# Down projections of two MLPs as Strassen products, with a ring of activation operands

## The chip, the cores and the metric

The kernel runs on one NeuronCore of one Trainium2 chip. The metric is the device time of one execution in microseconds. The kernel before took 3331.81 us (median of 3 runs, 3323.62 to 3334.83).

## The reference

A trunk of two layers over 1024 tokens and 16 learned tokens in front, 1040 in all, with 1024 features in float32. Each layer adds a token mixer to the residual stream (gated DeltaNet in the first, mLSTM in the second) and then an MLP:

```python
def squared_relu_mlp(h, w_up, w_down):
    a = jax.nn.relu(h @ w_up)
    return (a * a) @ w_down
...
        h = h + mix
        h = h + squared_relu_mlp(rms_norm(h, ffn_norm[layer]), ff_up[layer], ff_down[layer])
    return h[:, N_META:]
```

`w_up` is 1024 x 4096 and `w_down` 4096 x 1024. The case is about `(a * a) @ w_down` of both layers.

## The kernel before

Everything is kept feature-major: a tile has 128 features on partitions and tokens along the free dimension. The residual stream `hT` is eight such tiles of 1040 tokens in SBUF. Tokens go by halves of 520 and groups of 260. A float32 product is three single-pass matmuls (`mm3`, L105 to L107): each operand is split as hi + lo, the cast to hi on ScalarE and the low part `x - hi` as a subtraction on VectorE or GpSimd, and hi hi + lo hi + hi lo is summed in PSUM.

The stages run in this order: DeltaNet, its output projection, MLP of layer 1 (up, then down), mLSTM, MLP of layer 2. The up projection (`Up`, L933) already works by Strassen-Winograd products: of 2 x 2 blocks seven products instead of eight, each with a sum of weight blocks and a sum of token blocks. Its weight operands are made by `operand` (sums on VectorE L962, cast on ScalarE L978, low part L980). In the first and last few turns of a stage the low part of four of the seven goes to GpSimd (`help`), in the others all are VectorE's. The squared activations go to DRAM, `d_a`, by pairs of feature tiles.

The down projection (`Down`, L1044) is a plain product. It goes over eight blocks of four feature tiles of the activations (`HB`). A tile of 1040 tokens is fetched to `a_st` and split into `act_hi` (ScalarE, L1064) and `act_lo` (VectorE, L1065). For each block and each pair of output tiles, weights of 512 KB are loaded and split (L124 on ScalarE, L125 on GpSimd), and for each output tile and token group twelve matmuls accumulate in one PSUM tile `ps_dn`, which VectorE adds to `hT` (L1084). The last block goes by halves of the tokens: in layer 1 each finished block of `hT` is squared for the next norm (`ToNorm`, L853 to L857) and a finished half is normalised (`apply`, L896 to L902); in layer 2 each finished tile is transposed and written out (`ToOut`, L1187 to L1191), and the first half is one group of 504 tokens, since the 16 learned ones are dropped.

The order on each engine comes from a scheduler that sorts the program's instructions by a model of their times; the program's own order is that of `weave`, one step of every background stream between two pieces of the matmul stream. Tiles are rotated by pools, so a buffer's next writer waits for its last reader.

Of the kernel before, what the change touches and what calls it, by code (L numbers as in the profile page):

```python
# [7 lines left out]
F32 = mybir.dt.float32  # L8
F32R = mybir.dt.float32r
# [21 lines left out]
HB = 4  # L31
ALL = [[(0, G), (G, G)], [(2 * G, G), (3 * G, G)]]
REAL = [[(META, HALF - META)], ALL[1]]
# [15 lines left out]
class Ctx:  # L49
# [52 lines left out]
# Products of float32 operands: each is split as x = hi + lo with 12-bit parts, and  # L102
# hi*hi + hi*lo + lo*hi carries float32's accuracy in three single-pass products.
# [29 lines left out]
def softplus_neg_abs(nc, t, x):  # L133
    """log1p(exp(-|x|)) = 2 atanh(e / (2 + e)) as its series; returned without the factor 2."""
# [59 lines left out]
class GDN:  # L194
    """Gated DeltaNet by halves of the tokens and pairs of value heads.

    With raw (unnormalised) k and q, rk = |k|^-1, the recurrence is solved for y, v_new = beta rk y:
      (I + A) y = v / rk - e^cum k S,   A_ij = (k_i k_j) beta_j rk_j^2 e^(cum_i - cum_j),  i > j
      o ~ e^cum q S + [(q_i k_j) beta_j rk_j^2 e^(cum_i - cum_j)] y
    The norm of q enters through the epsilon of the output's RMS norm alone.  # L200
    Matrices over token pairs are held as [j, i].
    """
# [72 lines left out]
    def norm_in(self):  # L275
        """RMS norm of the first half's tokens."""
# [27 lines left out]
    def h_init(self, cc):  # L304
        """The residual stream of a chunk, feature-major, and the second half's sums of squares."""
# [35 lines left out]
    def norm_pair(self, j):  # L341
        """RMS norm of two feature tiles of the second half."""
# [87 lines left out]
    def column(self, s, ct, out):  # L430
        """Projection, convolution and SiLU of 128 features."""
# [60 lines left out]
    def prep(self, s, idx):  # L492
# [4 lines left out]
        # token-major k, and the norms of k and q  # L497
# [40 lines left out]
        # strictly upper 16 x 16 diagonal blocks, then their inverses by back substitution  # L538
# [13 lines left out]
        # token-major v / rk  # L552
# [22 lines left out]
        # merges 16 -> 32 -> 64 -> 104: with P' = B12^T L1, U12 = -P'^T U2, L = U^T  # L575
# [59 lines left out]
    def scan(self, s):  # L635
# [16 lines left out]
        for ci in range(HC):  # L652
# [31 lines left out]
            # -o, and its RMS norm  # L684
# [77 lines left out]
class OutUnits:  # L762
    """Output projection of the GDN layer, by halves of the tokens and of the heads."""
# [75 lines left out]
class Norm:  # L839
    """RMS norm over the features of the feature-major residual stream, sums of squares kept as it is made."""  # L840

    def __init__(self, c, pool, nw, ss=None):
        self.c, self.nc, self.pool, self.nw = c, c.nc, pool, nw
        self.ss = pool.tile([P, T], F32, tag="ss", name="ss") if ss is None else ss
        self.x, self.summed = [None, None], None
# [3 lines left out]
    def square(self, d, t0, n):  # L849
        nc, ss = self.nc, self.ss[:, t0:t0 + n]  # L850
        x = self.c.hT[:, d, t0:t0 + n]
        if d == 0:
# [6 lines left out]
    def sums(self, hf):  # L859
        """1 / rms of the tokens of a half, with tokens on partitions."""  # L860
# [9 lines left out]
    def rms(self, hf):  # L870
        """1 / rms of the tokens of a half, on all partitions."""
# [4 lines left out]
        r = self.pool.tile([P, 2, G], F32, tag="r", name="nr", bufs=1)  # L876
# [9 lines left out]
    def apply(self, hf, pool):  # L886
        """The normalised tokens of a half as an operand's two parts, by pairs of feature tiles."""
# [46 lines left out]
class Up:  # L934
    """relu(W_up^T x)^2 of all tokens, kept in DRAM, by Strassen-Winograd products: pairs of feature tiles of
    the result, of halves of the contraction and of token groups, a = [f, k] blocks and b = [k, t] blocks."""
    # product, its operand of the tokens
# [17 lines left out]
    def operand(self, raw, name, help):  # L955
        """A block of the weights, or a sum of blocks, as its two parts; the sums take the places of blocks."""
# [26 lines left out]
    def evac(self, i, hs, name, ps, tmp):  # L983
        """u: a11 b11, then the result's common part, then that of its second column; v: that of its second row."""
# [32 lines left out]
    def run(self, jobs):  # L1017
        """jobs: (pair of feature tiles, halves of the tokens, whether GpSimd helps, what to do first)."""
# [25 lines left out]
class Down:  # L1044
    """The residual stream plus W_down^T of the activations, over blocks of HB feature tiles."""

    def __init__(self, c, w_down, acts, after, spans):
        self.c, self.nc, self.w, self.acts, self.after, self.spans = c, c.nc, w_down, acts, after, spans
        self.a, self.pools, self.next = {}, [], []

    def open(self, st, side):
        self.pools.append(self.c.pool(f"acts{len(self.pools)}", HB, st, side=side))

    def fetch(self, j):
        st = self.c.row(j % 2, "a_st")
        self.nc.sync.dma_start(out=st, in_=self.acts[j // 2][:, j % 2].rearrange("p a b c -> p (a b c)"))
        self.next.append(st)

    def load(self, j):
        """A feature tile of the activations as its two parts."""  # L1060
        nc = self.nc
        st = self.next.pop(0)
        hi, lo = self.a[j] = pair(self.pools[j // HB % 2])
        nc.scalar.copy(hi.rearrange("p a b -> p (a b)"), st)  # L1064
        nc.vector.tensor_tensor(lo.rearrange("p a b -> p (a b)"), st, hi.rearrange("p a b -> p (a b)").bitcast(F32),  # L1065
                                op=ALU.subtract)
        if j + 1 < FF // P:
            self.fetch(j + 1)

    def tiles(self, b, dd, parts, last):  # L1070
        nc, c, hT = self.nc, self.c, self.c.hT
        whi, wlo = load_split(c, self.w[b * HB * P:(b + 1) * HB * P, dd * 256:(dd + 1) * 256].rearrange(
            "(h p) f -> p h f", p=P), [P, HB, 256])
        for d2 in range(2):
            d = dd * 2 + d2
            fs = slice(d2 * P, (d2 + 1) * P)
            for hf in parts:
# [545 lines left out]
```

## Time and profile before

| | |
|---|---|
| median of 3 runs | 3331.81 us (3323.62 to 3334.83) |
| span of the profiled execution | 3327.5 us |
| TensorE busy | 3149.4 us, 95% |
| VectorE busy | 1952.4 us, 59% |
| ScalarE busy | 1515.9 us, 46% |
| GpSimd busy | 980.2 us, 29% |
| down projection, layer 1 | 1671 to 2045 us |
| down projection, layer 2 | 2953 to 3321 us |

The profile is of one execution; its span goes from the first to the last instruction, and what lies around it is under the spread of the runs. Engines are PE (TensorE), PEld (its weight loads), DVE (VectorE), ACT (ScalarE), POOL (GpSimd) and SP (the queue of most DMAs). Busy times of operations overlap a little on VectorE, where one starts before the last has ended: the distance between starts is what an operation costs.

### The profile page before, as it was taken

To read this page: it belongs to the slowest core of one execution; us is meant where nothing else is said; L and a number is where in the kernel's file an instruction comes from. 1 tells how busy PE (TensorE), PEld (TensorE's weight loads), DVE (VectorE), ACT (ScalarE), POOL (GpSimd) and SP (SyncE) were. 2 spreads that over 40 slices of the span, in tenths; PEclk is the share of its full clock that TensorE was granted. 3 is DMA by queue.
4 is the path that set the end of the run, shared out by engine and by line. 5 is a ranking of instruction groups with operands and counts; after the bars stand their busy time and mean duration, and the time that the engine had idled before them with its cause. 6 is when DMAs were issued, how large, how long until landed. Compare 5 with 4: busy or idle time off the path is not lost.

```text
span 3327.5 us, 67692 instructions
## 1 busy us (share of the span) xinstructions
PE 3149.4 (95%) x27430; PEld 2981.0 (90%) x27430; DVE 1952.4 (59%) x4336; ACT 1515.9 (46%) x3547; POOL 980.2 (29%) x824
## 2 busy tenths in 40 slices
PE   7899998999999998899999998999999799999999
PEld 6898887888898898899999998988988799999998
DVE  6777668686676547876644437232336977553332
ACT  4565566656665543555521114433334455541112
POOL 4544444343443434200122224211123400022222
PEclk9999999999999999999999999999999999999999
DMA  3232222232223472343433222211132244343323
GB/s 95 70 85 79 68 76 81 67 91 66 80 74 94 143 213 71 115 131 115 130 115 99 90 65 70 63 52 48 47 90 59 82 132 125 106 144 96 96 90 96
DMA packets 398218, 308.87 MB, mean 93 GB/s; under 512 B 29201, under 2 KB 365242, under 8 KB 397906
## 3 DMA queue, kind: packets, MB, share of 16 engines
q1 hardware_dynamic: 362333, 270.44, 28.0%
q10 hardware_dynamic: 35573, 34.10, 3.0%
q8 instruction: 216, 3.54, 0.4%
q14 instruction: 96, 0.79, 0.1%
HBM read 245.88 MB, written 58.61 MB: 92 GB/s over the span
## 4 chain that ended last, share of the span: by engine, by line
PE 50%; DVE 5%; DMA 1%; ACT 1%; issue 1%; POOL 0%; SPq 0%; DVEq 0%; ACTq 0%; POOLq 0%
PE ps_dn L105 7%; PE ps_dn L107 7%; PE ps_dn L106 7%; PE ps_up L105 6%; PE ps_up L106 6%; PE ps_up L107 6%; PE ps_m L105 2%; PE ps_m L106 2%; PE ps_m L107 2%; PE mpo L1415 1%; PE mpo L1414 1%; DVE ss L857 1%; PE mpk L1377 1%; PE ps_mo L105 1%; PE ps_mo L107 1%
## 5 line engine op out<-in xcount | busy, mean ns | idle before, releaser
L125 POOL TENSOR_TENSOR wlo<-wraw,whi 128x1024 fp32r<-128x1024 f32 (+1 forms) x248 | 599.6, 2418 | 1134.6 <-ACT whi L124 1092.8
L105 PE MATMUL ps_dn<-act_hi,whi 128*128 128x260 f32 (+1 forms) x1792 | 536.7, 300 | 1.3 <-DVE hT L1084 1.2
L105 PE MATMUL ps_up<-xhi,uop 128*128 128x260 f32 x1792 | 511.4, 286 | 27.7 <-DVE up_u L991 10.0
L106 PE MATMUL ps_dn<-act_lo,whi 128*128 128x260 f32 (+1 forms) x1792 | 534.6, 298 | 0.0
L107 PE MATMUL ps_dn<-act_hi,wlo 128*128 128x260 f32 (+1 forms) x1792 | 533.6, 299 | 0.1
L107 PE MATMUL ps_up<-xhi,uop 128*128 128x260 f32 x1792 | 508.6, 284 | 3.2 <-DVE uop L980 3.2
L106 PE MATMUL ps_up<-xlo,uop 128*128 128x260 f32 x1792 | 510.4, 285 | 0.9 <-POOL xlo L927 0.9
L105 PE MATMUL ps_in<-act_hi,whi 128*128 128x260 f32 x1536 | 458.7, 299 | 15.2 <-ACT sz L489 12.4
L124 ACT CAST whi<-wraw 128x1024 fp32r<-128x1024 f32 (+1 forms) x248 | 255.8, 1032 | 472.5 <-PE ps_dn L106 359.9
L106 PE MATMUL ps_in<-act_lo,whi 128*128 128x260 f32 x1536 | 457.7, 298 | 0.0
L107 PE MATMUL ps_in<-act_hi,wlo 128*128 128x260 f32 x1536 | 452.8, 295 | 0.6 <-POOL wlo L125 0.5
L1084 DVE TENSOR_TENSOR hT<-hT,ps_dn 128x260 f32<-128x260 f32 (+1 forms) x448 | 204.5, 461 | 423.3 <-PE ps_dn L107 423.0
L105 PEld LDWEIGHTS ps_up<-xhi,uop 128*128 128x128 f32 x1792 | 341.4, 191 | 31.9 <-ACT uop L978 10.9
L105 PEld LDWEIGHTS ps_dn<-act_hi,whi 128*128 128x128 f32 x1792 | 337.5, 188 | 13.1 <-issue 1.3
L107 PEld LDWEIGHTS ps_dn<-act_hi,wlo 128*128 128x128 f32 x1792 | 338.3, 189 | 11.0 <-POOL mV L1293 0.3
L106 PEld LDWEIGHTS ps_dn<-act_lo,whi 128*128 128x128 f32 x1792 | 338.7, 189 | 10.5
L107 PEld LDWEIGHTS ps_up<-xhi,uop 128*128 128x128 f32 x1792 | 341.2, 191 | 3.8 <-DVE uop L980 3.6
L106 PEld LDWEIGHTS ps_up<-xlo,uop 128*128 128x128 f32 x1792 | 341.6, 191 | 1.4 <-POOL xlo L927 1.3
L105 PEld LDWEIGHTS ps_in<-act_hi,whi 128*128 128x128 f32 x1536 | 297.0, 193 | 21.1 <-ACT sz L489 14.4
L106 PEld LDWEIGHTS ps_in<-act_lo,whi 128*128 128x128 f32 x1536 | 297.2, 193 | 3.9 <-issue 0.2
L107 PEld LDWEIGHTS ps_in<-act_hi,wlo 128*128 128x128 f32 x1536 | 296.7, 193 | 3.9 <-POOL wlo L125 1.1
L105 PE MATMUL ps_m<-act_hi,whi 128*128 128x260 f32 x768 | 224.2, 292 | 5.6 <-ACT mso L1340 2.4
(386 smaller groups left out, 7064.0 us busy)
## 6 DMA issues: line engine op xcount, KB each, us to landing
wraw<-in_gdn_in_dram SPq DMA_DIRECT2D x96, 512.0 KB
wraw<-in_ff_down_dram SPq DMA_DIRECT2D x72, 512.0 KB
a_st<-d_a SPq DMA_DIRECT2D x64, 520.0 KB
d_a<-up_c ACTq DMA_DIRECT2D x88, 260.0 KB
wraw<-in_ff_up_dram SPq DMA_DIRECT2D x42, 512.0 KB
r<-in_ff_up_dram SPq DMA_DIRECT2D x42, 512.0 KB
wraw<-in_gdn_out_dram SPq DMA_DIRECT2D x32, 512.0 KB
wraw<-in_mlstm_in_dram SPq DMA_DIRECT2D x28, 512.0 KB
```

The source lines that it names most:

```text
L105: nc.tensor.matmul(ps, whi, xhi, start=first, stop=False)
L106: nc.tensor.matmul(ps, whi, xlo, start=False, stop=False)
L107: nc.tensor.matmul(ps, wlo, xhi, start=False, stop=last)
L124: nc.scalar.copy(hi, raw)
L125: (lo_engine or nc.gpsimd).tensor_tensor(lo, raw, hi.bitcast(F32), op=ALU.subtract)
L857: nc.vector.tensor_tensor(ss, ss, sq, op=ALU.add)
L1084: nc.vector.tensor_tensor(hT[:, d, t0:t0 + n], hT[:, d, t0:t0 + n], ps, op=ALU.add)
L1377: nc.tensor.matmul(pk[:, i], k[sl, c0 + i], q[sl, c0 + i], start=True, stop=True)
L1414: nc.tensor.matmul(po[:, 0], q[sl, ci], C[sl], start=True, stop=True)
L1415: nc.tensor.matmul(po[:, 1], E[hf][:, j, ci], V[:, ci, j], start=True, stop=True)
```

## The change

Both down projections now go by the same seven products. The contraction (32 feature tiles) is cut into 16 pairs `k`, the output into four pairs `j` of feature tiles (`PAIRS`), the tokens into pairs of groups in each half `hf`. For a pair `k` and a half, `feed` makes seven activation operands: the three blocks that are used as they are and four differences `dt` (VectorE, L1116), each with hi (ScalarE, L1129 to L1132) and lo (VectorE). They stand in a ring of four pairs per half (`RING`). A *turn* is one `j` with two or three pairs `k` (`UPTO`): it loads two rows of weights, makes seven weight operands (sums on VectorE L1162, cast on ScalarE L1177, low part on GpSimd L1178), and runs seven products of two or three `mm3` each. The first and the last round of four `j` go by halves of the tokens, one turn for each, so each makes its operands twice; the four rounds between take both halves in a turn. That is 32 turns of 7 weight operands per layer, 133 operands of 384 columns and 91 of 256. Every product is added from PSUM to `hT` or to a common part `z` (L1223 to L1228); `z` is added to three blocks of `hT` at the end (L1231, L1233). In the second layer all 1040 tokens are computed.

Beside it: six PSUM banks for `ps_dn` instead of four, the norms' bank closed during the stage; the first three pairs of the first half are fed during the last turns of the up projection; the next norm's scratch and the output rows lie in the two row tiles that held other things; the sums of squares start at the first block finished instead of feature tile 0; pools on other sides.

```diff
-    def tiles(self, b, dd, parts, last):
...
-                for t0, n in self.spans[hf]:
-                    gs = slice(t0 - hf * HALF, t0 - hf * HALF + n)
-                    ps = self.psum.tile([P, 512], F32, tag="pj", name="ps_dn")[:, :n]
-                    for j in range(HB):
-                        hi, lo = (x[:, hf, gs] for x in self.a[b * HB + j])
-                        mm3(nc, ps, whi[:, j, fs], wlo[:, j, fs], hi, lo, j == 0, j == HB - 1)
-                    nc.vector.tensor_tensor(hT[:, d, t0:t0 + n], hT[:, d, t0:t0 + n], ps, op=ALU.add)
...
+    RING = 4
+    PAIRS = KT // 2
+    UPTO = (2, 2, 3, 3, 4, 5, 6, 6, 7, 8, 9, 9, 10, 11, 11, 12, 13, 14, 14, 14, 16, 16, 16, 16)
+    OPERAND = {"a11": 0, "a12": 1, "s2": 4, "s3": 5, "s1": 3, "a22": 6, "s4": 2}
+    BANK = {"a11": "x", "a12": "x", "s3": "y", "a22": "y", "s1": "v", "s4": "v", "s2": "u"}
+    BOTH = ("a11", "s3", "a12", "s1", "a22", "s2", "s4")
+    ONE = ("a11", "s3", "s1", "s2", "a12", "a22", "s4")
...
+        for r, upto in enumerate(rounds):
+            split = r in (0, len(rounds) - 1)
+            for parts in ((0,), (1,)) if split else ((0, 1),):
+                for j in range(n):
+                    self.turns.append((j, at[j], upto[j], parts))
+            at = list(upto)
...
+    def feed(self):
...
+        for i, (k, hf) in enumerate(self.loads):
+            if i + 1 < len(self.loads):
+                self.fetch(i + 1)
+            b1, b2 = (r[:, i % 2] for r in self.rows)
+            t = self.dt.tile([P, 4, G], F32, tag="dt", name="dt")
+            sub(t[:, 0], b1[:, 1], b1[:, 0])
+            sub(t[:, 2], b2[:, 1], b1[:, 1])
+            yield
+            sub(t[:, 1], b2[:, 1], t[:, 0])
+            sub(t[:, 3], b2[:, 0], t[:, 1])
...
+            nc.scalar.copy(hi[:, 3:7], t)
+            sub(lo[:, 0], b1[:, 0], hi[:, 0].bitcast(F32))
+            sub(lo[:, 1:3], b2, hi[:, 1:3].bitcast(F32))
+            yield
+            sub(lo[:, 3:5], t[:, 0:2], hi[:, 3:5].bitcast(F32))
+            yield
+            sub(lo[:, 5:7], t[:, 2:4], hi[:, 5:7].bitcast(F32))
...
+    def operand(self, i, name):
...
+        if name == "s3":
+            x = sub(self.dm.tile([P, 3, P], F32, tag="s3", name="s3")[:, :kb], a11, a21)
+            self.raws[i].append(x)
+        elif name == "s1":
+            x = sub(a21, a21, a22, ALU.add)
+        elif name == "s2":
+            x = sub(a11, a22, self.raws[i][4])
+        elif name == "s4":
+            x = sub(a12, a12, a11)
...
+        nc.scalar.copy(w[:, 0:kb], x)
+        nc.gpsimd.tensor_tensor(w[:, kb:2 * kb], x, w[:, 0:kb].bitcast(F32), op=ALU.subtract)
...
+    def product(self, i, u, hf):
...
+        for k in range(kb):
+            hi, lo = (x[:, self.OPERAND[name]] for x in self.x[k0 + k, hf])
+            nc.tensor.matmul(ps, w[:, k], hi, start=begins and k == 0, stop=False, skip_group_check=True)
+            nc.tensor.matmul(ps, w[:, k], lo, start=False, stop=False, skip_group_check=True)
+            nc.tensor.matmul(ps, w[:, kb + k], hi, start=False, stop=k == kb - 1, skip_group_check=True)
...
+            if name == "a11" and k0 == 0:
+                nc.scalar.copy(z, ps)
+            else:
+                nc.vector.tensor_tensor(z, z, ps, op=ALU.add)
+        else:
+            out = place(d, t)[2]
+            nc.vector.tensor_tensor(out, out, ps, op=ALU.add)
...
+        for i, (j, k0, k1, parts) in enumerate(self.turns):
+            while self.todo < len(self.loads) and self.need[self.todo] <= i:
+                next(self.feeder)
...
+            for u in range(7):
+                self.ahead(i, u, 3)
+                for hf in parts:
+                    self.product(i, u, hf)
+                    if self.todo < len(self.loads) and self.room[self.todo] <= i:
+                        next(self.feeder)
...
-        down.psum = c.pool("pd", 4, pst, space=PSUM)
+        down.psum = c.pool("pd", 6, pst, space=PSUM)
```

How the instructions move is seen at two places of layer 1. First VectorE in the middle of the down projection. Before, about one block (`hT` are the evictions, `act_lo` the low parts of the activations):

```order
L1084 TENSOR_TENSOR hT<-hT,ps_dn 128x260 x27
L1065 TENSOR_TENSOR act_lo<-a_st,act_hi 128x1040 x2
L1084 TENSOR_TENSOR hT<-hT,ps_dn 128x260 x4
L1065 TENSOR_TENSOR act_lo<-a_st,act_hi 128x1040
L1084 TENSOR_TENSOR hT<-hT,ps_dn 128x260
```

And now, a part of one turn (`dt` and `dlo` are a pair's differences and low parts, `s`, `r` and `wraw` the weight sums):

```order
L1225 TENSOR_TENSOR z<-z,ps_dn 128x260
L1162 TENSOR_TENSOR s_23499<-wraw,r_23441 128x384
L1225 TENSOR_TENSOR z<-z,ps_dn 128x260
L1162 TENSOR_TENSOR r_23441<-r_23441 128x3x128
L1228 TENSOR_TENSOR hT<-hT,ps_dn 128x260
L1116 TENSOR_TENSOR dlo<-a_st,dhi 128x260
L1116 TENSOR_TENSOR dlo<-a_st,dhi 128x520
L1162 TENSOR_TENSOR wraw<-wraw 128x3x128
L1228 TENSOR_TENSOR hT<-hT,ps_dn 128x260
L1116 TENSOR_TENSOR dlo<-dt,dhi 128x520 x2
L1116 TENSOR_TENSOR dlo<-a_st,dhi 128x260
L1225 TENSOR_TENSOR z<-z,ps_dn 128x260
```

Where runs of up to 27 evictions followed each other with a few low parts between, evictions, weight sums and activation operands now alternate. Second GpSimd, from the end of the up projection into the down projection. Before (`uop` are low parts of the up projection, `wlo` of the down weights, 35 in a row):

```order
L980 TENSOR_TENSOR uop<-s_21322,uop 128x512
L980 TENSOR_TENSOR uop<-r_21262,uop 128x512
L980 TENSOR_TENSOR uop<-wraw,uop 128x512
L125 TENSOR_TENSOR wlo<-wraw,whi 128x1024
L1293 MEMSET mV_26441 104x10
L1293 MEMSET mV_26442 104x10
L125 TENSOR_TENSOR wlo<-wraw,whi 128x1024 x35
```

And now, with the first turn's seven operands `dop` and the first of the second's:

```order
L979 TENSOR_TENSOR uop<-s_21324,uop 128x512
L979 TENSOR_TENSOR uop<-r_21257,uop 128x512
L979 TENSOR_TENSOR uop<-wraw,uop 128x512
L1178 TENSOR_TENSOR dop<-wraw,dop 128x256
L1178 TENSOR_TENSOR dop<-s_21527,dop 128x256
L1178 TENSOR_TENSOR dop<-r_21522,dop 128x256
L1178 TENSOR_TENSOR dop<-wraw,dop 128x256 x2
L1178 TENSOR_TENSOR dop<-r_21522,dop 128x256
L1178 TENSOR_TENSOR dop<-wraw,dop 128x256
L1178 TENSOR_TENSOR dop<-s_21612,dop 128x256
```

36 long subtractions in the stage have become 224 short ones, each of which a product waits for.

## Rows read from the trace of the kernel before

**Rows 1.** The page, parts 1 and 4: busy time by engine, chain.

```profile
PE 3149.4 (95%) x27430; PEld 2981.0 (90%) x27430; DVE 1952.4 (59%) x4336; ACT 1515.9 (46%) x3547; POOL 980.2 (29%) x824
...
PE 50%; DVE 5%; DMA 1%; ACT 1%; issue 1%; POOL 0%; SPq 0%; DVEq 0%; ACTq 0%; POOLq 0%
```

**Rows 2.** Windows of both down stages: PE, PEld, DVE, ACT, POOL busy; clock, DMA.

```profile
1671.00:2045.00 374.00, 370.92 (x3076) 370.03 (x3076) 158.95 (x307) 76.65 (x99) 91.19 (x39) 1.00 0.28 88
...
2953.00:3321.00 368.00, 367.88 (x2375) 334.93 (x2374) 129.96 (x220) 75.43 (x87) 89.11 (x36) 1.00 0.32 99
```

**Rows 3.** Windows inside up (first two) and down, columns the same.

```profile
1327.00:1380.00 53.00, 41.00 (x292) 39.21 (x291) 52.17 (x73) 28.55 (x59) 26.95 (x15) 0.90 0.29 88
1400.00:1600.00 200.00, 200.00 (x1672) 200.00 (x1672) 134.08 (x221) 108.82 (x196) 0.00 (x0) 1.00 0.42 128
1700.00:2000.00 300.00, 300.00 (x2502) 300.00 (x2502) 114.82 (x233) 52.86 (x53) 66.14 (x26) 1.00 0.27 86
3000.00:3250.00 250.00, 250.00 (x1599) 227.36 (x1598) 95.00 (x157) 46.50 (x46) 58.70 (x23) 1.00 0.30 94
```

**Rows 4.** Groups by line at 1700:2000: count, busy us, mean ns, idle before.

```profile
L1084 DVE TENSOR_TENSOR hT<-hT,ps_dn 128x260 f32<-128x260 f32 x208 | 87.4, 425 | 179.7 <-PE ps_dn L107 179.6
L125 POOL TENSOR_TENSOR wlo<-wraw,whi 128x1024 fp32r<-128x1024 f32 x26 | 66.1, 2544 | 233.4 <-ACT whi L124 233.4
```

**Rows 5.** Groups of PE at 3000:3250, one of three lines per width.

```profile
L105 PE MATMUL ps_dn<-act_hi,whi 128*128 128x260 f32 x354 | 100.2, 283 | 0.0
...
L106 PE MATMUL ps_dn<-act_lo,whi 128*128 128x504 f32 x179 | 70.1, 392 | 0.0
```

**Rows 6.** Timeline of VectorE: start us, duration us, operation.

```profile
1341.80 1.50 DVE L922 TENSOR_TENSOR st_t<-st_b 128x260 f32<-128x260 f32 x1
1343.22 0.41 DVE L991 TENSOR_TENSOR up_c<-up_v,ps_up 128x260 f32<-128x260 f32 x1
1343.55 0.68 DVE L962 TENSOR_TENSOR wraw<-r,s 128x512 f32<-128x512 f32 x1
1344.15 0.68 DVE L962 TENSOR_TENSOR r<-r 128x512 f32<-128x512 f32 x1
1344.76 0.42 DVE L923 TENSOR_TENSOR st_t<-st_b,st_t 128x260 f32<-128x260 f32 x1
1345.10 0.41 DVE L991 TENSOR_TENSOR up_c<-up_u,ps_up 128x260 f32<-128x260 f32 x1
```

**Rows 7.** Timeline of GpSimd at the same place.

```profile
1341.71 1.30 POOL L980 TENSOR_TENSOR uop<-s,uop 128x512 fp32r<-128x512 f32 x1
```

**Rows 8.** Lines L980 and L125 on GpSimd: duration ns minimum/median/maximum.

```profile
L980 POOL TENSOR_TENSOR uop<-wraw,uop x20: 1285/1304/2263, 1319.4 to 2950.4; 128x512 fp32r<-128x512 f32 x20
...
L125 POOL TENSOR_TENSOR wlo<-wraw,whi x248: 1830/2391/3638, 18.2 to 3308.4; 128x1024 fp32r<-128x1024 f32 x116, 128x768 fp32r<-128x768 f32 x8
```

**Rows 9.** Groups of VectorE at 1327:1380: four of its 19.

```profile
L919 DVE SCALAR_TENSOR_TENSOR st_b<-hT,ncols,nr 128x520 f32<-128x520 f32 x8 | 7.8, 1010 | 0.4 <-ACT nr L883 0.4
L980 DVE TENSOR_TENSOR uop<-wraw,uop 128x512 fp32r<-128x512 f32 x7 | 6.3, 907 | 0.1
...
L922 DVE TENSOR_TENSOR st_t<-st_b 128x260 f32<-128x260 f32 x3 | 4.0, 1332 | 0.0
...
L991 DVE TENSOR_TENSOR up_u<-up_u,ps_up 128x260 f32<-128x260 f32 x6 | 2.5, 413 | 0.2 <-PE ps_up L107 0.2
```

**Rows 10.** Groups of GpSimd at 1327:1380: two of its four.

```profile
L927 POOL TENSOR_TENSOR xlo<-st_b,xhi 128x780 fp32r<-128x780 f32 x4 | 10.6, 2648 | 5.7 <-ACT xhi L926 5.7
L980 POOL TENSOR_TENSOR uop<-wraw,uop 128x512 fp32r<-128x512 f32 x5 | 7.4, 1470 | 6.0 <-ACT uop L978 6.0
```

**Rows 11.** Windows in the same stretch, columns as in rows 2.

```profile
1350.00:1355.00 5.00, 0.60 (x6) 0.41 (x5) 5.00 (x5) 1.36 (x2) 5.00 (x3) 0.91 0.82 230
1355.00:1360.00 5.00, 5.00 (x23) 5.00 (x24) 5.00 (x11) 0.62 (x1) 0.65 (x1) 0.50 0.02 5
```

**Rows 12.** Waits at 1671:2045: us in total, times, longest us.

```profile
ACT act_hi L1064 <- DMA a_st<-d_a: 26.7, 12, 3.6
```

More of the change, by code (lines that the diff above doesn't have):

```diff
@@ L851, in square @@
         x = self.c.hT[:, d, t0:t0 + n]
-        if d == 0:
+        if t0 not in self.seen:
+            self.seen.add(t0)
             nc.scalar.activation(ss, x, AF.Square)
@@ L1044 @@
 class Down:
[L1047 to L1057, printed above, removed]
@@ L1091, in run @@
-    def run(self):
-        nb = FF // P // HB
-        for b in range(nb - 1):
-            for dd in range(KT // 2):
-                self.load((b + 1) * HB + dd)
-                yield from self.tiles(b, dd, (0, 1), False)
-        self.after.begin(self.pools)
-        for hf in range(2):
-            for dd in range(KT // 2):
-                yield from self.tiles(nb - 1, dd, (hf,), True)
-            self.after.half(hf)
-def mlp(c, w_up, w_down, norm, spans, sides, xa, st, acts, after, closed):
-    down = Down(c, w_down, acts, after, spans)
+    RING = 4
@@ new lines, in open @@
+    def open(self):
+        c = self.c
+        self.dt = c.pool("dt", 2, self.st[0], side=self.sides[0])
+        self.xp = [c.pool("dx0", self.RING, self.st[0], side=self.sides[0])]
+        self.rows = [c.row(s, "a_st").rearrange("p (a b c) -> p a b c", a=2, b=2) for s in range(2)]
+        self.fetch(0)
+        self.feeder = self.feed()
+        self.ready = max(i for i, (k, hf) in enumerate(self.loads) if hf == 0 and self.need[i] < self.PAIRS) + 1
+        assert all(hf == 0 for _, hf in self.loads[:self.ready])
@@ new lines, in ahead @@
+    def ahead(self, i, u, by):
+        while len(self.made) <= 7 * i + u + by and self.next[0] < len(self.turns):
+            ti, tu = self.next
+            if tu == 0:
+                for r in range(2):
+                    if len(self.raws.get(ti, ())) <= 2 * r:
+                        self.load_w(ti, r)
+            self.made.append(self.operand(ti, self.names(self.turns[ti])[tu]))
+            if tu == 2 and ti + 1 < len(self.turns):
+                self.load_w(ti + 1, 0)
+            if tu == 6 and ti + 1 < len(self.turns):
+                self.load_w(ti + 1, 1)
+            self.next = (ti, tu + 1) if tu < 6 else (ti + 1, 0)
@@ new lines, in run @@
+    def run(self):
+        c, n = self.c, self.PAIRS
+        self.dm = c.pool("dm", 1, self.st[1], side=self.sides[1])
+        self.xp.append(c.pool("dx1", self.RING, self.st[1], side=self.sides[1]))
+        self.z = self.dm.tile([P, n, 2, G], F32, name="z")
+        self.nop, self.made, self.next, self.banks = 0, [], (0, 0), {}
+        for i, (j, k0, k1, parts) in enumerate(self.turns):
+            while self.todo < len(self.loads) and self.need[self.todo] <= i:
+                next(self.feeder)
+            ends = k1 == FF // P // 2
+            if ends and parts == (0,) and j == 0:
+                self.after.begin()
+            for u in range(7):
+                self.ahead(i, u, 3)
+                for hf in parts:
+                    self.product(i, u, hf)
+                    if self.todo < len(self.loads) and self.room[self.todo] <= i:
+                        next(self.feeder)
+                    yield
+            if ends:
+                for d in range(2):
+                    self.after.row(2 * j + d, parts[0])
+                if j == n - 1:
+                    self.st[parts[0]].close()
+                    self.after.half(parts[0])
@@ L1108, in mlp @@
+def mlp(c, w_up, w_down, norm, sides, xa, acts, after, closed):
+    down = Down(c, w_down, acts, after, sides)
     n, e = FF // P // 2, 3
@@ L1116, in first_done @@
             closed()
-            down.open(st, sides[0])
-            down.fetch(0)
-            for j in range(HB):
-                down.load(j)
+            down.open()
+            c.bg.append(down.first())
         jobs = [(i, (0,), True, None) for i in range(e)]
@@ L1534, in run @@
         self.nst, self.xa, self.pst = nst, ExitStack(), ExitStack()
-        c.acts = c.pool("macts", 5, self.acts_st)
+        c.acts = c.pool("macts", 5, self.acts_st, side="right")
         n = self.NH // 2
```

161 lines of the change are left out of this document (115 added, 46 removed).

## The prediction

> **What bounds the kernel now.** I read the busy shares first, then the chain of waits, then the busy time by stage. TensorE is busy 95% of the span and has half of the chain, ten times the next engine's share [rows 1]. The two down projections are the windows 1671 to 2045 us (374 us) and 2953 to 3321 us (368 us): TensorE has 370.9 and 367.9 us of work in them, at a granted clock of 1.00, while VectorE has 159 and 130 us and GpSimd 91 and 89 us [rows 2]. Inside, nothing makes TensorE wait: from 1700 to 2000 it runs 2502 passes in 300 us, 0.1199 us each (0.1196 in the up projection: 1672 in 200) [rows 3]; I use 0.1195. The evictions wait for TensorE, not it for them: before 208 of them VectorE idles 179.6 us for its products [rows 4]. In layer 2, whose first half drops 16 tokens, a pass has 504 or 260 columns: 1062 of 260 and 537 of 504 fill 250 us [rows 3, 5], so a pass of 504 takes (250 - 1062 x 0.1195) / 537 = 0.229 us.
>
> **What the change removes.** A down projection now takes 3072 passes of 260 columns (layer 1: 367 us) or 1536 of 260 with 768 of 504 (layer 2: 359 us). Afterwards both take 2688 of 260 columns: 321 us. TensorE's work falls by 46 and 38 us, 84 us together. That is the whole gain on offer, and the question is what the two engines that now feed TensorE ask for it.
>
> **What it adds.** First the prices. VectorE issues back to back: after an operation of 260 columns the next starts 0.33 to 0.34 us later, after one of 512 it starts 0.60 us later [rows 6] (the 0.41 and 0.68 us in the rows are latencies that overlap). So 260 columns (and 256) cost 0.335, 384 cost 0.47 and 520 cost 0.615 us. GpSimd's subtraction takes 1.285 us for 512 columns and 1.83 us for 768 (the minima in [rows 8]), 2.13 ns a column: 0.74 us for 256 columns, 1.01 us for 384.
>
> Per layer the list of the changed kernel has:
> - GpSimd: 7 low parts in each of 32 turns, 133 of 384 and 91 of 256 columns: 134.3 + 67.3 = 202 us (before: 90 us).
> - VectorE, both inputs in SBUF: 32 loads of a pair (4 differences, 1 low part of 260, 3 of 520) at 3.52 us = 113 us, three of them before the stage begins; weight sums 76 x 0.47 + 52 x 0.335 = 53 us; closing sums 8 x 0.95 = 7.6 us. Together 173 us.
> - VectorE from PSUM: 328 evictions x 0.335 = 110 us.
>
> Each engine alone fits beside TensorE's 321 us. Together GpSimd and the SBUF part of VectorE do not, for they exclude each other. A VectorE subtraction of 260 columns that starts at 1341.80, when a GpSimd operation has just begun (1341.71, 1.30 us), takes 1.50 us and not 0.42: it ends 0.3 us after GpSimd's [rows 6, 7]. The one at 1344.76, with GpSimd idle, takes 0.42. Evictions from PSUM aren't held up: all 208 in [rows 4] mean 425 ns with GpSimd running 66 us beside them.
> The Trainium skill (SBUF — State Buffer, Who interferes with whom) has this as a rule: a VectorE instruction with two SBUF inputs and a GpSimd instruction that reads SBUF exclude each other for the whole instruction, and one with at most one SBUF input is free; the rows agree, and the rule speaks against a change that puts 202 us on one and 173 us on the other.
>
> How tightly the two pack is seen at 1327 to 1380, where the up projection's low parts go to GpSimd [rows 3, 9, 10]. VectorE has there 27 operations of 512 columns, 12 of 260, 8 of 520 with a scalar (0.64), 3 of 1040 (1.17) and 1 of 520, 29.5 us, and GpSimd 11 x 1.285 + 4 x 1.86 = 21.5 us: 51 us of a 53 us stretch. The 21 evictions (7 us) lie beside GpSimd but for about 1.2 us. TensorE is busy 41 of the 53 us. So a stage takes the sum of both engines' SBUF work plus a share of its evictions; I take a quarter, a little worse than here, since evictions are half of the queue now and stand between waits.
>
> By rounds of the list of turns (time = larger of TensorE and SBUF sum + a quarter of the evictions):
> - First round, each half alone, pairs 2, 2, 3, 3 per turn: GpSimd 49.0, sums 12.9, six loads 21.1: 83 us, + 4 (48 evictions) = 87. TensorE needs 50.
> - Four middle rounds, 45 pairs: GpSimd 107.4, sums 28.5, 23 loads 81: 217 us, + 19 (224 evictions) = 236. TensorE 226.
> - Last round, each half alone, 3, 2, 2, 2: GpSimd 45.2, sums 11.8, closing 7.6: 64.6 us, + 4.7 = 69. Layer 1 adds 28 sums of squares (9.4 us) and the norm of the first half (13 us: 8 x 0.68, 4 x 0.615, 4 x 1.3): 92. TensorE 45.
>
> Layer 1: 415 us for 374; layer 2: 392 for 368. That is 41 + 24 = +65 us.
>
> Seams. The second row of weights of the first turn goes where the up projection's buffers were, so its load waits for that stage, and the second product for load, difference, cast and low part: 2.2 us (a load waited for here: 26.7 us in 12 waits, [rows 12]) + 0.4 + 0.5 + 0.74, less the first product's 0.7: +3, at most 4.5 with the longest wait of 3.6. I take +5 a layer, with the buffers' own release; below nothing it can't go, since TensorE passes this seam without a gap now. At the end two feature tiles are transposed and written instead of one: +2 us. Sum: +77 us on a span of 3327.5 us, whose run lies in the middle of the three shown (3323.6 to 3334.8); on their median 3331.8 that makes **3408 us**.
>
> Costed at nothing: two more PSUM banks, the norm's scratch and output rows in other tiles, ScalarE's casts (some 170 us a layer, in the shadow of a 390 us stage), and DMA. The weights are read 83 / 64 as often (the two split rounds read theirs twice), 21.8 MB for 16.8, beside 17 MB of activations: the DMA share goes from 0.28 [rows 2] to about 0.3. On SP's queue a fetch of activations waits for a load two earlier to be used up by VectorE, and the next turn's weights stand behind it; while VectorE is the late one this costs only what is already counted. If that cover were gone, each of 32 turns could lose a wait of 2.2 us, 70 us a layer; that is inside the rival of late evictions below.
>
> Clock: after 5 us in which TensorE worked 0.6 us it ran the next 5 us at 0.50, 1.2 GHz [rows 11]. In the two split rounds TensorE has 95 us of work in 156 to 179 us. Even at half clock it needs 190: at most some 30 us a layer, kept for the upper end.
>
> **Rivals.**
> - TensorE stays the bound (the other side). If VectorE and GpSimd always found each other's gaps, TensorE's 84 us come out, less 12 us of seams: 3260 us. For it: each engine alone has time, and the middle rounds' SBUF sum (217) is just under TensorE's 226. Against: the split rounds' sums are 83 and 65 to 87 where TensorE needs 50 and 45, and at 1327 to 1380 TensorE did wait. It decides if the split rounds come in below 60 us.
> - GpSimd holds VectorE for half of its operation only. GpSimd's terms halve: first round 62, middle 226, last 66 (layer 1) and 47: 354 and 335 us, -53 + 12, 3291 us. Against: the row at 1341.80 waited to the end.
> - Evictions come late. VectorE works in order: an eviction behind a subtraction that waits for GpSimd holds a PSUM bank, TensorE stops, GpSimd's next operand isn't released. With no eviction hidden the stages take 497 and 474 us (+229); halfway, 0.6 exposed, +150: 3480 us. For it: six banks serve eight names, and VectorE's list alternates evictions and SBUF operations where it had 27 evictions in a row. Against: the 1.2 of 7 us above.
>
> **How the numbers follow.** Forecast 0.58, late evictions 0.20, half hold 0.12, TensorE the bound 0.10. What a measurement of this kernel can tell from no change is 0.3%, 10 us. Faster by more: the last two but for their upper edge, 0.20. Within: that edge and the forecast's lowest, 0.08. Slower: 0.72. Both signs have weight, so the likeliest's own range is said: 3359 (no eviction exposed, the middle at TensorE's pace, no seams) to 3450. The whole range goes from 3305, which leaves out TensorE as the bound and part of the half hold, to 3475, which leaves out the worse half of the late evictions.
>
> **What would show it.** Right: in both down stages TensorE busy well under its window, first and last rounds worst; VectorE busy over 90%, its SBUF subtractions at means far above 0.42 and 0.69 us while evictions stay at 0.42; GpSimd's 384 columns at 1.0 us or more, and GpSimd over 200 us busy in each stage. Wrong: TensorE at 0.12 us a pass throughout with stages of about 330 us, or VectorE's subtractions at their undisturbed times while GpSimd runs.

## The result, and the profile after

The changed kernel takes 3417.14 us (median of 4 runs, 3416.28 to 3419.21) where the kernel before takes 3327.72 in the runs beside it (3323.26 to 3334.83): a ratio of 1.0259, 95% interval 1.024 to 1.0277. The profiled run's span is 3415.7 us for 3327.5. The forecast was 3408, slower.

Busy time by engine, from the page of the changed kernel; [rows 1] are those of before:

```profile
PE 3139.0 (92%) x27430; PEld 2967.2 (87%) x27430; DVE 2425.4 (71%) x5280; ACT 1692.3 (50%) x4067; POOL 1261.1 (37%) x1200
```

TensorE's busy time falls by 10 us only, though its passes fall by some 84 us: the ends of matmuls are modelled and part of the work ran at a lower granted clock (0.96 in the stages below, 1.00 in [rows 2]), so its busy share is no measure of the gain. VectorE gains 473 us and GpSimd 281.

By the starts of the matmuls of each stage, the two down projections take 417.6 and 405.9 us for 376.2 and 367.2 (+41 and +39), the two up projections 353.7 and 352.2 for 347.4 and 349.1 (+6 and +3), and all the rest together -1. The windows of both down stages, to be held against [rows 2]; columns are the window, its length, then busy time and count of PE, PEld, DVE, ACT and POOL, then clock, DMA share and GB/s:

```profile
1671.00:2093.00 422.00, 369.11 (x2771) 351.60 (x2770) 386.63 (x737) 173.88 (x367) 242.40 (x229) 0.96 0.31 91
3000.00:3409.00 409.00, 364.44 (x2775) 349.54 (x2773) 363.79 (x700) 164.12 (x345) 232.17 (x225) 0.96 0.34 98
```

VectorE is now busy for 92% and 89% of a stage in which it had work for 43% and 35%. By rounds (first, the four in the middle, last; layer 1, then layer 2), the same columns:

```profile
1674.70:1762.90 88.20, 68.11 (x423) 60.58 (x422) 76.87 (x135) 40.31 (x90) 60.35 (x58) 0.88 0.38 114
1762.90:2012.10 249.20, 235.03 (x1893) 230.93 (x1892) 228.02 (x457) 93.39 (x178) 121.91 (x112) 0.99 0.32 93
2012.10:2092.60 80.50, 61.86 (x427) 55.99 (x426) 79.47 (x141) 37.73 (x95) 58.13 (x58) 0.94 0.22 63
3002.70:3093.40 90.70, 66.31 (x422) 59.60 (x421) 77.05 (x134) 40.34 (x90) 58.86 (x58) 0.89 0.36 111
3093.40:3347.90 254.50, 238.13 (x1892) 233.98 (x1891) 229.21 (x457) 93.39 (x178) 123.86 (x112) 0.97 0.31 91
3347.90:3408.90 61.00, 57.25 (x442) 53.22 (x440) 56.25 (x106) 28.32 (x74) 47.97 (x54) 1.00 0.40 112
```

The forecast had 87, 236 and 92 (layer 2: 69). What VectorE does with the time is in its groups in the middle rounds of layer 1 (form, count, busy us, mean ns, idle before):

```profile
L1228 DVE TENSOR_TENSOR hT<-hT,ps_dn 128x260 f32<-128x260 f32 x159 | 63.4, 413 | 13.7 <-PE ps_dn L1210 13.6
L1178 POOL TENSOR_TENSOR dop<-wraw,dop 128x384 fp32r<-128x384 f32 x53 | 60.1, 1141 | 64.9 <-ACT dop L1177 64.7
L1116 DVE TENSOR_TENSOR dlo<-dt,dhi 128x520 fp32r<-128x520 f32 x42 | 35.7, 886 | 0.5 <-ACT dhi L1132 0.5
L1116 DVE TENSOR_TENSOR dt<-a_st 128x260 f32<-128x260 f32 x42 | 22.2, 552 | 0.2 <-DMA a_st<-d_a 0.2
L1116 DVE TENSOR_TENSOR dlo<-a_st,dhi 128x260 fp32r<-128x260 f32 x22 | 18.1, 824 | 0.1
```

Evictions take their 413 ns; a subtraction of the same 260 columns with both inputs in SBUF takes 552 to 824. One place shows why. VectorE from 1832.65 (start us, us, operation):

```profile
1832.65 0.75 DVE L1228 TENSOR_TENSOR hT<-hT,ps_dn 128x260 f32<-128x260 f32 x2
1833.33 0.89 DVE L1116 TENSOR_TENSOR dt<-a_st 128x260 f32<-128x260 f32 x1
1834.14 0.41 DVE L1228 TENSOR_TENSOR hT<-hT,ps_dn 128x260 f32<-128x260 f32 x1
1834.48 0.90 DVE L1116 TENSOR_TENSOR dt<-a_st 128x260 f32<-128x260 f32 x1
1835.30 0.42 DVE L1116 TENSOR_TENSOR dt<-a_st,dt 128x260 f32<-128x260 f32 x1
```

and GpSimd's two low parts in the same stretch, one row:

```profile
1832.92 2.16 POOL L1178 TENSOR_TENSOR dop<-wraw,dop 128x384 fp32r<-128x384 f32 x2 [2.04 <-ACT dop L1177]
```

GpSimd runs from 1832.92 to 1835.08. The two subtractions that start meanwhile take 0.89 and 0.90 us, the evictions among them no longer than elsewhere; the next one, after GpSimd's end, takes 0.42. That is [rows 6, 7] again, now through the whole stage.

An account of VectorE in these middle rounds can be worked out. Its own price per instruction is 65 ns and 1.04 ns a column (that gives the 0.335 and 0.60 us of [rows 6]): 74.6 us of evictions and 103.0 us of SBUF work. It is busy for 228.0 us and idle for 21.2. What its own work leaves of the 228.0, 50.4 us, is time in which an instruction stood longer than its price: held. Not all of it is GpSimd's, since an operation before a gap shows its whole 0.41 us: the same account leaves 8.6 us in the run without GpSimd's reads below. GpSimd's own work there, by 195 ns and 2.13 ns a column, is 107.5 us, so well over half of it fell beside evictions and idle time.

How the two engines share a round can be read from the starts and ends of their instructions: the time in which GpSimd or an SBUF operation of VectorE is under way, the time in which an eviction is and neither of these, and the time in which both engines stand still (us):

| round (layer 1, layer 2) | GpSimd or SBUF work | eviction alone | neither |
|---|---|---|---|
| first | 79.7, 80.3 | 4.2, 4.8 | 4.3, 5.5 |
| middle four | 204.5, 204.7 | 33.0, 35.7 | 11.7, 14.1 |
| last | 74.6, 56.5 | 5.6, 4.0 | 0.2, 0.5 |

In the split rounds GpSimd's and VectorE's SBUF work fill nine tenths of the time, and of some 16 to 20 us of evictions 4 to 6 stand alone. In the middle rounds 33.0 and 35.7 of 74.6 do. The first column is 6 to 8 us below the sum of both engines' prices (87.7, 210.4 and 82.8 us in layer 1), so the two overlap a little.

TensorE's waits in the middle rounds of layer 1 (us in total, times, longest) are evictions that come late:

```profile
PE ps_dn L1208 <- DVE z L1225: 8.7, 7, 2.5
PE ps_dn L1208 <- DVE hT L1228: 4.0, 5, 2.0
PE ps_dn L1208 <- ACT dop L1177: 0.7, 1, 0.7
```

The two waits for evictions, 12.7 us, are a good half of the 23 us by which these rounds exceed TensorE's 226 (layer 2: 14.8 of 28); most of the rest does not show as a wait of TensorE.

### The profile page after: what moved, and what is told of

It is laid out like the page before. It is cut to its first block, busy times and chain, and to the rows that moved or that the text cites. A ratio compares the mean times of both kernels' runs of the same rounds, so it can differ in the third digit from the quotient of the medians.

```text
span 3415.7 us, 70131 instructions
## 1 busy us (share of the span) xinstructions
PE 3139.0 (92%) x27430; PEld 2967.2 (87%) x27430; DVE 2425.4 (71%) x5280; ACT 1692.3 (50%) x4067; POOL 1261.1 (37%) x1200
## 5 line engine op out<-in xcount | busy, mean ns | idle before, releaser
L122 POOL TENSOR_TENSOR wlo<-wraw,whi 128x1024 fp32r<-128x1024 f32 (+1 forms) x176 | 418.8, 2380 | 582.3 <-ACT whi L121 560.2
L1208 PE MATMUL ps_dn<-dhi,dop 128*128 128x260 f32 x1792 | 528.8, 298 | 84.9 <-ACT dop L1177 34.4
L1209 PE MATMUL ps_dn<-dlo,dop 128*128 128x260 f32 x1792 | 514.7, 289 | 0.0
L1210 PE MATMUL ps_dn<-dhi,dop 128*128 128x260 f32 x1792 | 504.1, 293 | 9.4 <-POOL dop L1178 8.7
L1208 PEld LDWEIGHTS ps_dn<-dhi,dop 128*128 128x128 f32 x1792 | 349.2, 195 | 107.7 <-ACT dop L1177 51.1
L1210 PEld LDWEIGHTS ps_dn<-dhi,dop 128*128 128x128 f32 x1792 | 342.5, 196 | 17.1 <-POOL dop L1178 16.0
L1209 PEld LDWEIGHTS ps_dn<-dlo,dop 128*128 128x128 f32 x1792 | 350.3, 196 | 0.0
L1178 POOL TENSOR_TENSOR dop<-wraw,dop 128x384 fp32r<-128x384 f32 (+1 forms) x256 | 265.8, 1046 | 209.8 <-ACT dop L1177 209.5
L1177 ACT CAST dop<-wraw 128x384 fp32r<-128x384 f32 (+1 forms) x256 | 118.8, 469 | 288.3 <-PE ps_dn L1210 186.0
L979 POOL TENSOR_TENSOR uop<-wraw,uop 128x512 fp32r<-128x512 f32 x20 | 30.1, 1505 | 563.6 <-ACT uop L977 298.6
```

The source lines that it names most:

```text
L122: (lo_engine or nc.gpsimd).tensor_tensor(lo, raw, hi.bitcast(F32), op=ALU.subtract)
L979: lo.tensor_tensor(w[:, 4:8], x, w[:, 0:4].bitcast(F32), op=ALU.subtract)
L1177: nc.scalar.copy(w[:, 0:kb], x)
L1178: nc.gpsimd.tensor_tensor(w[:, kb:2 * kb], x, w[:, 0:kb].bitcast(F32), op=ALU.subtract)
L1208: nc.tensor.matmul(ps, w[:, k], hi, start=begins and k == 0, stop=False, skip_group_check=True)
L1209: nc.tensor.matmul(ps, w[:, k], lo, start=False, stop=False, skip_group_check=True)
```

## The experiments

All are the changed kernel with one to four edits, and every ratio is to the kernel before on the same chip (medians 3330.8 to 3331.5).

**Low parts of the weights on VectorE.**

```diff
-        nc.gpsimd.tensor_tensor(w[:, kb:2 * kb], x, w[:, 0:kb].bitcast(F32), op=ALU.subtract)
+        nc.vector.tensor_tensor(w[:, kb:2 * kb], x, w[:, 0:kb].bitcast(F32), op=ALU.subtract)
```

> All low parts of the down weights on VectorE, none on GpSimd (224 per layer). Theory A, GpSimd and VectorE exclude each other's SBUF work: GpSimd's 202 us leave the sum and 93 us come to VectorE; with no GpSimd to hide beside, every eviction counts. First round 34 + 22 + 16 = 73 us (now 88 to 91), middle 110 + 50 + 75 = 234 (now 249 to 254), last 59 in layer 2 (now 61) and about 80 in layer 1 (now 80): 387 and 366 us, 3417 - 70 = 3347 us, with VectorE's SBUF operations at their undisturbed 0.41 and 0.69 us. Theory B, VectorE's own volume is the bound whatever GpSimd does: 93 us more in each layer, 3600 us. Theory C, the latency from sum over cast and low part to TensorE with four operand buffers is the bound: the low part takes 0.47 instead of 1.0 us, stages near TensorE's 321 us, about 3300 us.

Measured: 3378.32 us, ratio 1.0148 (1.0127 to 1.0168): 39 us less than the changed kernel, though VectorE has some 90 us more of its own to do per layer. So it is not VectorE's volume by itself that made the change slow (B), and C's 3300 is missed by more than A's 3347, which is 31 us too low. First and middle rounds of layer 1:

```profile
1678.60:1759.70 81.10, 64.49 (x423) 57.65 (x421) 76.70 (x192) 40.80 (x90) 0.00 (x0) 0.89 0.41 123
1759.70:2000.80 241.10, 233.07 (x1892) 229.28 (x1891) 230.44 (x568) 93.30 (x178) 0.00 (x0) 0.99 0.32 95
```

VectorE is busy 95% of both: by the same prices 74 us of evictions and 152 us of SBUF work in the middle, 226 in 241.1, as much as TensorE has (226). Two engines that feed each other in order, both with 226 us of work, take 241. A took the larger of the two in each round (73, 234) and had no term for their waits on each other: the first rounds came out 8 and 9 us above it, the middle ones 7 and 6.

**GpSimd without its reads.** The instructions stay with VectorE and ScalarE as they are; GpSimd subtracts 16 columns and writes constants to the rest.

```diff
-        nc.gpsimd.tensor_tensor(w[:, kb:2 * kb], x, w[:, 0:kb].bitcast(F32), op=ALU.subtract)
+        lo = w[:, kb:2 * kb].rearrange("p a b -> p (a b)")
+        nc.gpsimd.tensor_tensor(w[:, kb, :16], x[:, 0, :16], w[:, 0, :16].bitcast(F32), op=ALU.subtract)
+        for m in (kb * P, kb * P * 2 // 3):
+            nc.gpsimd.memset(lo[:, 16:m].bitcast(F32), 0.0)
```

> GpSimd subtracts only 16 columns of each low part and then writes constants with two memsets of 1 and 2/3 of the operand, so that it takes about as long as before (0.8 and 0.95 us) behind the same wait, but reads next to nothing. Leaves out the rest of the low parts. Theory A (exclusion by reading SBUF): VectorE's subtractions return to 0.42 and 0.69 us, stages at the larger of TensorE and VectorE: first 52, middle 230, last 50 to 65: about 347 and 332 us, 3417 - 145 = 3272 us. Theory B (VectorE's volume) and theory C (length of the operand's chain): nothing is taken from VectorE or from the chain, 3417 us.

Measured: 3308.87 us, ratio 0.9941 (0.9918 to 0.9964): 108 us below the changed kernel and below the kernel before. Middle rounds:

```profile
1746.40:1975.80 229.40, 226.96 (x1893) 226.50 (x1892) 185.53 (x456) 92.77 (x177) 110.17 (x336) 1.00 0.33 100
```

and the low parts of 520 columns on VectorE there (form, count, busy, mean):

```profile
L1116 DVE TENSOR_TENSOR dlo<-dt,dhi 128x520 fp32r<-128x520 f32 x42 | 27.4, 692 | 0.2 <-ACT dhi L1132 0.2
```

GpSimd is busy for 110 us (122 in the changed kernel), yet the middle rounds run nearly at TensorE's pace, and the subtractions take 692 ns for 886. A shorter way of the operand (C) is not the reason: from the end of a cast to the end of GpSimd's last instruction on that operand the median is 2.35 us in these rounds, for 1.18 in the changed kernel. The exclusion is therefore shown: same work on VectorE, nearly the same occupation of GpSimd, and 108 us of the time gone with GpSimd's reads. The Trainium skill (SBUF — State Buffer, Who interferes with whom) says that a GpSimd instruction which only writes SBUF does not contend with a VectorE instruction with two SBUF inputs; these 692 ns agree. What is missing to A's 3272 lies in the split rounds: the first ones take 67.3 and 69.8 us where TensorE has 50. In layer 1's it waits 9.9 us there, 6.8 of them for casts, and its granted clock is 0.92.

**Low parts shared between both.** GpSimd keeps three of seven operands.

```diff
-        nc.gpsimd.tensor_tensor(w[:, kb:2 * kb], x, w[:, 0:kb].bitcast(F32), op=ALU.subtract)
+        lo = nc.gpsimd if name in ("a12", "a22", "s4") else nc.vector
+        lo.tensor_tensor(w[:, kb:2 * kb], x, w[:, 0:kb].bitcast(F32), op=ALU.subtract)
```

> Four of seven low parts (a11, s3, s1, s2) on VectorE, three (a12, a22, s4) on GpSimd. Theory A: first 68 + 6 = 74, middle: SBUF sum 184, VectorE's own 213 plus some 18 of GpSimd in its way, 231; last 59 and 78: 383 and 364 us, 3417 - 77 = 3340 us; as all on VectorE, or a little under, since evictions can hide beside what GpSimd keeps. Theory B: 53 us more a layer, 3523 us. Theory C: half the way to a short chain, about 3370 us.

Measured: 3402.63 us, ratio 1.0217 (1.0194 to 1.0239). All theories missed: A by 63 us, C by 33, B by 120. Middle rounds of layer 1:

```profile
1765.70:2010.50 244.80, 233.94 (x1892) 229.50 (x1892) 232.15 (x521) 93.05 (x178) 54.20 (x48) 0.99 0.32 95
```

The SBUF sum is small here (132 us on VectorE, 45 on GpSimd), but VectorE is again busy 95%: 206 us of its own, 26 held. A's sum of SBUF work with a quarter of the evictions is not the rule of the middle rounds; VectorE's own queue, lengthened by what GpSimd holds it, is. Nearly half of A's miss lies in the first rounds, though: 88.7 and 87.0 us for the 74 expected, no less than in the changed kernel. VectorE is busy there for 79.5 of 88.7 us, 65.7 of its own and 13.8 held, and why it stands idle for the other 9 is left open.

**First round not split by token halves**, so that each weight operand is made once there.

```diff
-            split = r in (0, len(rounds) - 1)
+            split = r == len(rounds) - 1
...
-        self.loads = sorted(first, key=lambda x: (first[x], x))
+        self.loads = sorted(first, key=lambda x: (first[x], x[1], x[0]))
...
-        self.ready = max(i for i, (k, hf) in enumerate(self.loads) if hf == 0 and self.need[i] < self.PAIRS) + 1
+        self.ready = max(i for i, (k, hf) in enumerate(self.loads) if hf == 0 and self.need[i] == 0) + 1
```

> The first round takes both halves of the tokens in a turn, so its operands are made once; only the last round is split. Low parts stay on GpSimd. Theory A: the first round falls from 83 + 4 to 25 + 6.5 + 25 + 4 = 60 us, less some 7 us of waiting for the second half's loads at the seam: 20 us a layer, 3377 us. Theory B: VectorE loses only 6.5 us of sums a layer, 3404 us. Theory C: 28 operands fewer in each layer at about 1.3 us, 3345 us.

Measured: 3370.26 us, ratio 1.0121 (1.0101 to 1.0142), as A said within 7 us. The first round of layer 1:

```profile
1671.00:1739.30 68.30, 58.07 (x422) 55.70 (x421) 60.33 (x119) 29.25 (x62) 30.68 (x30) 0.90 0.34 102
```

20 us less than the split one (layer 2: 25 less), at GpSimd's half of the work. Some of it is paid back: the second round takes 65.7 us for 61.5, since operands move into it. The seam into the stage shrinks too: in the changed kernel TensorE waits once for 5.6 us on the first ScalarE casts, here for 2.5 us in two waits.

**Both: low parts on VectorE, first round whole.**

> All low parts of the weight operands on VectorE, and the first round not split by token halves (each operand built once there). A (the port shared by VectorE and GpSimd, then a full VectorE queue): in the first round VectorE has 46 us of its own in the run with the whole round and 12 us of low parts come to it, with 8 us idle about 66 us, for 82 with low parts on VectorE and a split round; the second round gets 4 us longer. 3378 - 2 x (16 - 4) - 10 (the stages of the up projections) = 3345, range 3330 to 3355. B (the low parts are what is late in the first round, however they are built: moving them and halving them are one gain, not two): 3368. C (both gains add in full, 3417 - 39 - 47): 3331.

Measured: 3342.32 us, ratio 1.0032 (1.0021 to 1.0043). A's 3345 holds. Within 11 us of the kernel before, but still above it. Middle rounds:

```profile
1737.10:1980.70 243.60, 233.09 (x1892) 228.19 (x1891) 233.71 (x574) 95.38 (x182) 0.00 (x0) 1.00 0.33 97
```

**Short evictions.**

```diff
-                nc.vector.tensor_tensor(z, z, ps, op=ALU.add)
+                nc.vector.tensor_tensor(z[:, :16], z[:, :16], ps[:, :16], op=ALU.add)
...
-            nc.vector.tensor_tensor(out, out, ps, op=ALU.add)
+            nc.vector.tensor_tensor(out[:, :16], out[:, :16], ps[:, :16], op=ALU.add)
```

> The changed kernel with evictions of 16 columns for 260 (0.08 us for 0.335 by the own time of VectorE); the sums of the other 244 columns are left out. A (the forecast's sum: SBUF work of VectorE and GpSimd, which exclude each other, and only a part of the evictions on top): the first round stays at 87 to 88 us, since 87.5 us of SBUF work fill it; the middle four rounds fall from 249 to TensorE's 226 to 230; the last stays near 80 and 61. About 3417 - 22 - 27 = 3368. Q (VectorE's queue in order: evictions count in full): the first round falls by 12 us to 76, the last by 14 to 66 and 50, the middle to 228: 3417 - 2 x 12 - 25 - 49 = 3321 or less. C (evictions cost nothing): 3417.

Measured: 3368.08 us, ratio 1.011 (1.0095 to 1.0125), on A's number, in part by luck: the middle rounds end 2 to 4 us above A's, the split ones 0 to 4 us below. First, middle and last rounds of layer 1:

```profile
1682.30:1766.00 83.70, 63.88 (x422) 58.59 (x421) 66.83 (x135) 40.19 (x90) 59.21 (x57) 0.88 0.40 119
1766.00:2000.40 234.40, 230.37 (x1893) 228.70 (x1891) 186.89 (x459) 93.30 (x180) 123.47 (x114) 0.99 0.33 99
2000.40:2077.20 76.80, 61.69 (x399) 56.17 (x400) 71.23 (x143) 37.84 (x95) 58.70 (x59) 0.87 0.20 58
```

The first round keeps 83.7 of its 88.2 us (layer 2: 88.3 of 90.7) although 12 us of evictions are gone. GpSimd or SBUF work of VectorE is under way for 79.6 us of it (80.6), as in the changed kernel (79.7 and 80.3): that work fills the round, and what fell away, 4.5 and 2.4 us, is about what evictions alone had taken (4.2 and 4.8). The middle falls by 15 us (layer 2: 22) for 56 us of evictions removed; there TensorE's 226 us are the next bound, so this is not all that they cost beside the SBUF work.

**Without reads, first round whole.**

> GpSimd subtracts 16 columns of each low part and fills the rest with constants (the rest of the low parts is left out), and the first round is not split. A (the port): nothing is left that holds VectorE up; TensorE's 50 us and the gap at the start set the first round, 56 for 67, the second gets 4 us longer: 3309 - 2 x 7 - 5 = 3290. B (halving the builds gained only through less exclusion, of which none is left): 3309. C (the 47 us of the whole round come in full): 3262.

Measured: 3285.67 us, ratio 0.9863 (0.9846 to 0.9881), as A. This is what the seven products give with the low parts left out: 45 us below the kernel before. Of TensorE's 84 us the rest, 39, is still lost: the first rounds take 61.9 and 64.8 us where TensorE has 50 (its granted clock there is 0.92 and 0.89), the last 59.2 and 53.1 for 45, the up stages +2 and +1.

**Low parts on VectorE, first round whole, short evictions.**

> Low parts on VectorE and the first round whole, with evictions of 16 columns for 260 (the sums of the other 244 columns are left out). V (VectorE's queue is full: busy 234 of 244 us in the middle rounds, where TensorE needs 226): evictions come off in full until TensorE is the bound; first round 65 to 58, middle 244 to 230, last 79 and 60 to 70 and 53 per layer: 3342 - 28 - 27 = 3287. T (what is left is TensorE's restarts and the chain through ScalarE, evictions cost nothing): 3335 to 3342.

Measured: 3288.31 us, ratio 0.9876 (0.9859 to 0.9894): V. The middle rounds:

```profile
1732.90:1960.50 227.60, 227.13 (x1891) 226.64 (x1891) 189.40 (x581) 95.63 (x182) 0.00 (x0) 1.00 0.35 105
```

With 56 us off VectorE, TensorE works all of its 227 us: in the run with everything on VectorE it is VectorE's full queue, and not TensorE's restarts or ScalarE's casts, that costs the last 16 us.

**One eviction for both token halves**, in the whole rounds (two neighbouring PSUM banks in one tile; of the edit the core).

```diff
+        if len(parts) == 2:
+            if hf == 0:
+                return
+            ps, z = self.pairs[name_bank], self.z[:, j]
...
-        down.psum = c.pool("pd", 6, pst, space=PSUM)
+        down.psum = c.pool("pd", 3, pst, space=PSUM)
```

> Low parts on VectorE, the first round whole, and one VectorE eviction of both token halves (2x260 columns, from two neighbouring PSUM banks) in place of two, in all rounds that are not split: 140 instructions fewer per layer, each some 0.065 us by the difference between twice the 260-column pitch (0.335) and the 520-column one (0.60). V (VectorE's queue is full): 9 us per layer, 3342 - 18 = 3324. L (the first half's bank comes free up to 1.1 us later, and TensorE waits for it): 3342 to 3360.

Measured: 3360.73 us, ratio 1.0089 (1.0075 to 1.0104): 18 us slower than without it. L at its upper edge, not V.

```profile
1744.80:1990.90 246.10, 232.68 (x1892) 229.12 (x1892) 227.61 (x466) 95.88 (x182) 0.00 (x0) 0.99 0.32 97
```

VectorE's work does fall, from 233.7 to 227.6 us busy, and the middle rounds get 2.5 us longer all the same: TensorE waits 10.1 us for evictions there (6.8 on `z`, 3.3 on `hT`; 7.4 without the edit). Three of the four halves of the last rounds lose 3 to 4 us as well, where two products now share a tile that comes free only after both: in layer 1's last round TensorE waits 14.9 us for evictions, 4.6 without the edit. The two stages are 15 us longer together; of the other 8 us between the two profiled runs 7 stand ahead of both stages, in work that the edit doesn't touch.

**That, and one low part of 1040 columns for two of 520.**

```diff
-            sub(lo[:, 3:5], t[:, 0:2], hi[:, 3:5].bitcast(F32))
-            yield
-            sub(lo[:, 5:7], t[:, 2:4], hi[:, 5:7].bitcast(F32))
+            sub(lo[:, 3:7], t, hi[:, 3:7].bitcast(F32))
+            yield
```

> As the run with paired evictions, and the low parts of the four activation sums in one instruction of 1040 columns in place of two of 520 (32 instructions fewer per layer, 2 us). V: 3320. L (a VectorE instruction of 1.15 us holds evictions up): as the run before it or up to 10 us more.

Measured: 3355.77 us, ratio 1.0075 (1.0062 to 1.0089). The interval overlaps the run before it; V's direction, but not told apart. No version that computes everything took less time than the kernel before.

## Why the prediction came out right, point by point

**The gain on offer.** 84 us of TensorE's passes was right, and the runs without GpSimd's reads show how much of it can come out: with TensorE as the bound the middle rounds take 229 us against 226 worked out.

**Exclusion.** Right, and shown from both sides: without GpSimd's reads 108 us go; with its work moved to VectorE 39 us go in spite of the added work. Subtractions of 260 columns at 552 to 824 ns and evictions at 413 were named beforehand as the sign. So was GpSimd's rate: 1141 ns at 384 columns, 242 and 232 us busy a stage. VectorE's share, expected above 90%, is 92% and 89%.

**First round.** 87 worked out, 88.2 and 90.7 measured, and its terms hold: 79.7 and 80.3 us of SBUF work for 83, and 4.2 and 4.8 us of evictions alone for the 4 that a quarter gives. The run with short evictions bears both out. What comes on top, 4.3 and 5.5 us in which neither engine works, is mostly the standstill at the start of the stage, which belongs to the seam.

**Middle rounds.** The step "I take a quarter" failed: 236 worked out, 249.2 and 254.5 measured. SBUF work takes 204.5 us (217 in the working), evictions alone 33.0 and 35.7 us, 44% and 48% of 74.6 and not a quarter, and for 11.7 and 14.1 us neither engine works, for which the sum had no term. The price came from a stretch with 21 evictions in 53 us; here there are 224 in 249, between subtractions that GpSimd holds, and VectorE takes them in order. The form of the rule was wrong as well: with 177 us of SBUF work, where a sum with a quarter of the evictions gives TensorE's 226, the shared run took 245. What bounds these rounds is VectorE's queue, its own work plus what it is held, and it costs time already when it comes near TensorE's own 226 us; the run with short evictions and all low parts on VectorE shows this, where 56 us off the queue bring the rounds to 227.6.

**Last round.** 92 and 69 worked out, 80.5 and 61.0 measured. The quarter holds here: 5.6 and 4.0 us of evictions alone for 4.7. Too large was the SBUF sum, 87 and 65 us for 74.6 and 56.5. By the prices of what ran it is 82.8 and 62.3 us, and the rest is that the two engines overlap by some 6 to 8 us a round, which the working left out. So the total is right in part by luck: middle and last errors cancel in layer 1 (+13, -12, with 1 us on the first round) and leave +14 us in layer 2 (392 worked out, 405.9 measured).

**Seams.** +5 each worked out, for the load of the second row of weights. That wait is there: TensorE's first wait for a cast, inside the first round, is 5.6 and 7.8 us, and for 2.8 and 4.4 us of it VectorE and GpSimd stand still as well. But the up stages grew too, by 6.3 and 3.1 us, of which 4.6 and 5.6 come in their last 190 passes, while three pairs are already fed; the working had put that feeding at nothing. So a seam cost 7 to 9 us. The first split rounds run at a granted clock of 0.88 and 0.89, and the first rounds of all variants between 0.83 and 0.95; this was kept for the upper end, and what it costs was not measured by itself. In the changed kernel SBUF work and evictions alone fill 84 of 88 us of that round, which leaves little for it. The tail took +0.3 and not +2.

**Rivals.** TensorE as the bound: only in runs that leave out GpSimd's reads or most of the evictions. Half hold: refuted by the subtractions that wait to GpSimd's end. Late evictions: in part, 12.7 and 14.8 us of waits in the middle rounds. On the span the sum is +88 us for +77: the middle rounds' +13 and +18, less the -12 and -8 of the last rounds, with some us from the first rounds and the seams.

## What to carry to other kernels

A product fewer on TensorE is paid in sums, casts and evictions on the engines beside it. Before making such a trade, add up VectorE's own queue, and separately VectorE's two-SBUF-input work together with GpSimd's reads; both have to stay clearly below TensorE's new time, since at 226 us each two engines needed 241 to 244. When GpSimd's share is what holds VectorE up, moving it onto VectorE (549 ns for 384 columns, where GpSimd took 1141) gained 39 us even with VectorE nearly full, and moving four operands of seven only 15.

## What the runs showed that I had not expected

- GpSimd busy for 110 of 229 us, most of it filling SBUF with constants, did not lengthen VectorE's subtractions (692 ns for 520 columns, for 886 beside GpSimd's subtractions).
- Merging two evictions into one took 6 us off VectorE in the middle rounds, and the two stages still got 15 us longer: the moment at which a PSUM bank comes free was worth more than VectorE's time.
- Two engines share badly: with three of seven low parts left on GpSimd the kernel takes 3402.6 us, much nearer to all seven there (3417.1) than to none (3378.3). Why its first rounds gain nothing stays open.
